# A two-layer diffusion trunk: layer 0's first feed-forward projection by seven block products instead of eight, with its results through DRAM

## The chip, the cores and the metric

The kernel runs on one core of a Trainium2 chip. The core has five engines with a queue of instructions each: TensorE (PE in the rows; its weight loads are PEld), VectorE (DVE), ScalarE (ACT), GpSimd (POOL), and SyncE (SP), which issues most DMAs. Matrix products land in PSUM (eight banks), everything else is in SBUF, inputs and outputs are in DRAM. The metric is the device time of one execution in microseconds, the median of several.

## The reference

Two layers over 512 latent and 256 context tokens of width 1024 (768 columns in the kernel, the context first). Layer 0 mixes by pooling and a recurrence, layer 1 by attention; each is followed by a SwiGLU feed-forward of hidden width 2816. Every sub-layer has a norm ahead and one behind, with shift, scale and gate worked out from the conditioning vectors `c` and `c_ctx` (the modulation). Only the latent rows are returned.

```python
def swiglu(h, w_in, w_out):
    a, b = jnp.split(h @ w_in, 2, axis=-1)
    return (jax.nn.silu(a) * b) @ w_out

for l in range(DEPTH):
    need_ctx = l < DEPTH - 1
    m_lat = (jax.nn.silu(c) @ ada_w[l] + ada_b[l])[:, None]
    m_ctx = jax.nn.silu(c_ctx) @ ada_w[l] + ada_b[l]
...
    x = x + g1 * rmsnorm(y_lat, norm_g[l, 1])
    f_lat = swiglu(rmsnorm(x, norm_g[l, 2]) * (1.0 + sc2) + sh2, ffn_w_in[l], ffn_w_out[l])
    x = x + g2 * rmsnorm(f_lat, norm_g[l, 3])
    if need_ctx:
        ctx_s = ctx_s + cg1 * rmsnorm(y_ctx, norm_g[l, 1])
        f_ctx = swiglu(rmsnorm(ctx_s, norm_g[l, 2]) * (1.0 + csc2) + csh2, ffn_w_in[l], ffn_w_out[l])
        ctx_s = ctx_s + cg2 * rmsnorm(f_ctx, norm_g[l, 3])
```

## The kernel before

Activations lie transposed: 128 features on the partitions, tokens along the row, eight tiles for the width of 1024 (index `k`). Each float32 operand of a large product is split into two float32r parts, a high one (`hi`, a rounding copy on ACT) and a low one (`lo`, the remainder, a subtraction on DVE; `split`, L570). A product of two split operands is three matmuls (`mm3`, L117: high by high, high by low, low by high), and the three lines L121 to L123 are nearly all of PE's work. Weights come from DRAM in halves of 128x1024 (`raw`, four buffers), are split into slots of 128x2048 (`w`, two of them, and `w3`, a third one in the feed-forward) and used at once.

The feed-forward of layer 0 (`ffn`, L599) goes through the 22 hidden blocks of 128 in chunks of 4, 4, 4, 4, 4 and 2 (`FCH`). A hidden block loads 128x2048 weights (the gate's half and the other one), and for the column groups 0 to 255 (context) and 256 to 767 (latent) makes two results over the eight `k` (2 x 24 matmuls for each group), a SiLU on ACT, a product on DVE and a split into tiles `gh`, `gl` in SBUF. At the end of a chunk the second projection multiplies its tiles by the weights `w_fo` and adds to the eight rows `y` (a copy on ACT for the first chunk, an addition on DVE later, L637). The first three blocks and the last two are made in groups of 256 columns, as the norms deliver or want them. The norms run beside the products as generators (`along`, `tick`): squares on ACT, sums on DVE, two small PE steps (L140, L155) with a power on POOL between them, then scaling on DVE and ACT, and the residual's addition on POOL.

Layer 1's modulation (`ada_cols`, L292) runs beside layer 0's feed-forward: 48 loads of 128x1024, and for each two DVE instructions of 1024 elements that also sum up (L297), one for the latent vector and one for the context's. After the last chunk come the last two norms of each column group, then `att_proj` (L680): queries and keys of layer 1, first for latent columns 0 to 255, then 256 to 511. The queries are written into tiles of the pool `y`.

The code names no times: a scheduler lays out each engine's queue ahead of the run, in order of the program with gaps filled. A queue is worked off in its order, and a waiting instruction holds back all behind it.

Of the kernel before, what the change touches and what calls it, by code (L numbers as in the profile page):

```python
# [15 lines left out]
D = 1024  # L16
# [16 lines left out]
FCH = (4, 4, 4, 4, 4, 2)  # L33
# [27 lines left out]
class Groups:  # L61


    def __init__(self, pool, groups):
        self.t = {}
        self.add(pool, groups)

    def add(self, pool, groups):
        for a, _ in groups:
            self.t[a // 256] = [pool.tile([128, 256], F32, tag=f"y{a // 256}_{k}", name=f"y{a // 256}_{k}") for k in range(KD)]  # L70

    def __call__(self, k, a, b):
        return self.t[a // 256][k][:, a % 256:a % 256 + b - a]
# [8 lines left out]
class Trunk:  # L82
    def __init__(self, tc, a, dbg=None, stop=None):
        self.tc, self.nc, self.a = tc, tc.nc, a
        self.dbg = dbg or {}
        self.stop = stop
        self.w3, self.nw = None, 0
# [17 lines left out]
    def wslot(self, src, n, pool=None, tag="w"):  # L105

        if pool is None:
            self.nw += 1
            pool, tag = (self.w3, "w3") if self.w3 and self.nw % 3 == 0 else (self.wp, "w")
        hi = pool.tile([128, 2048], F32R, tag=tag + "hi", name=tag + "hi")  # L110
        lo = pool.tile([128, 2048], F32R, tag=tag + "lo", name=tag + "lo")
# [5 lines left out]
    def mm3(self, out, ops, first=True, last=True):  # L117

        n = len(ops)
        for i, (wh, wl, xh, xl) in enumerate(ops):  # L120
            self.nc.tensor.matmul(out=out, lhsT=wh, rhs=xh, start=first and i == 0, stop=False)  # L121
            self.nc.tensor.matmul(out=out, lhsT=wh, rhs=xl, start=False, stop=False)  # L122
            self.nc.tensor.matmul(out=out, lhsT=wl, rhs=xh, start=False, stop=last and i == n - 1)  # L123
# [50 lines left out]
    def prenorm(self, x, h, l, which, a, b):  # L174
# [8 lines left out]
        for k in range(KD):  # L183
# [13 lines left out]
    def norm(self, x, a, b):  # L197

        ss = yield from self.sumsq(x, a, b)
        rb = self.spread(self.rms(ss, b - a, D))  # L200
        for k in range(KD):
            self.nc.vector.tensor_tensor(out=x(k, a, b), in0=x(k, a, b), in1=rb[:, :b - a], op=ALU.mult)

    def modulate(self, x, h, l, which, a, b):
# [3 lines left out]
        for k in range(KD):  # L208
            u = self.np.tile([128, 256], F32, tag="u", name="u", bufs=8)
            nc.vector.tensor_scalar(out=u[:, :n], in0=x(k, a, b), scalar1=self.scol[l][which][:, k, c:c + 1],  # L210
                                    scalar2=self.shcol(l, which, k, c), op0=ALU.mult, op1=ALU.add)
            nc.scalar.activation(out=h[0](k, a, b), in_=u[:, :n], func=AF.Copy)
            (nc.gpsimd if k % 2 else nc.vector).tensor_tensor(out=h[1](k, a, b), in0=u[:, :n],
                                                              in1=h[0](k, a, b).bitcast(F32), op=ALU.subtract)
# [47 lines left out]
    def htiles(self, ctx=True):  # L262
        return [cols(self.hcp if ctx else None, self.hlp, KD, F32R, t) for t in ("hh", "hl")]
# [28 lines left out]
    def ada_cols(self, m):  # L292

        nc = self.nc
        raw = self.load(self.a["adat"][m], 1024)
        for i in range(2):
            nc.vector.scalar_tensor_tensor(out=self.junk, in0=raw, scalar=1.0, in1=self.cb[:, i * 1024:i * 1024 + 1024],  # L297
# [4 lines left out]
    def load_cb(self, cb):  # L302
        self.cb = cb
        self.nc.sync.dma_start(out=cb, in_=self.a["cb"].partition_broadcast(128))
        self.nc.scalar.activation(out=cb, in_=cb, func=AF.Silu)

    def ada_tail(self, l, m0, m1, src):
# [3 lines left out]
        nc.vector.tensor_tensor(out=m[:, m0:m1, :], in0=src,  # L311
                                in1=self.adab[:, l * 48 + m0:l * 48 + m1].unsqueeze(2).to_broadcast([128, m1 - m0, 2]),
                                op=ALU.add)
        for o in range(m0, m1, 8):
            which, part = divmod(o // 8, 3)
            ng = self.ng[:, (l * 4 + which * 2) * 8:(l * 4 + which * 2 + 2) * 8]
            if part == 1:
                nc.vector.scalar_tensor_tensor(out=self.scol[l][which], in0=m[:, o:o + 8, :], scalar=1.0,
                                               in1=ng[:, 0:8].unsqueeze(2).to_broadcast([128, 8, 2]),
                                               op0=ALU.add, op1=ALU.mult)  # L320
            elif part == 2:
                nc.vector.tensor_tensor(out=self.gcol[l][which], in0=m[:, o:o + 8, :],
                                        in1=ng[:, 8:16].unsqueeze(2).to_broadcast([128, 8, 2]), op=ALU.mult)
# [275 lines left out]
    def ffn(self, l, y, h, order0, groups, last, done, step=0):  # L599


        nc = self.nc
        j0, slot = 0, 0
        for ci, kc in enumerate(FCH):
            g = [cols(self.gp if l == 0 else None, self.gp, kc, F32R, t) for t in ("gh", "gl")]
            w = {}

            def load(i):
                if i not in w:
                    w[i] = self.wslot(self.a["w_fi"][l, j0 + i], 2048)  # L610
                    self.ada_steps(step if ci == 1 else 0)
# [526 lines left out]
```

## Time and profile before

| | |
|---|---|
| median of 3 runs (lowest, highest) | 1637.59 us (1635.88, 1639.59) |
| the profiled execution: its time, its span | 1640.13 us, 1638.2 us |
| mean granted clock of PE | 0.989 of full |
| busy share of PE, PEld, DVE, ACT, POOL | 96%, 84%, 57%, 36%, 7% |
| matmuls | 10920 |
| DRAM traffic | 158.35 MB read, 5.24 MB written |

A matmul's busy time covers its whole passage, and the next one starts before it ends: that PE is busy says that it does not wait, and what a matmul costs is the distance from its start to that of the next. Times of the text lie on the profiled execution's axis.

### The profile page before, as it was taken

What the parts mean: (1) busy time and instruction counts of PE and PEld (TensorE: products, weight loads), DVE (VectorE), ACT (ScalarE), POOL (GpSimd) and SP (SyncE); (2) the same over time, 40 slices, a digit from 0 to 9 for tenths busy, and PEclk for the clock granted to TensorE, in tenths of its full rate; (3) what the DMA queues carried; (4) which work ended last, traced back from release to release, by engine and by line L of the source; (5) the groups of instructions that cost most, each with busy time, mean ns of one, the idle gap of its engine ahead of it and who ended that gap; (6) DMA issues with size and microseconds to landing.
All of it is one profiled execution on the core that took longest, in us unless ns stands there. A gap on an engine that the chain in (4) does not pass through costs nothing.

```text
span 1638.2 us, 26865 instructions
## 1 busy us (share of the span) xinstructions
PE 1571.3 (96%) x10920; PEld 1377.5 (84%) x10920; DVE 931.6 (57%) x1821; ACT 587.4 (36%) x1104; POOL 112.1 (7%) x147
## 2 busy tenths in 40 slices
PE   4999999999999999999999999899999999999997
PEld 1877777789998888888888898899998888888886
DVE  5466575654656566676532458778937523343345
ACT  4334343254542211212122135458845332222222
POOL 1100000001200000000000012310004000000002
PEclk9999999999999999999999999999999999999999
DMA  9242232342215444444421113230032223322311
GB/s 339 79 155 79 82 126 79 123 153 85 86 56 164 129 144 152 142 142 153 130 65 65 53 52 104 71 110 27 1 104 78 93 88 103 103 92 89 103 52 52
DMA packets 55803, 167.96 MB, mean 103 GB/s; under 512 B 7040, under 2 KB 16000, under 8 KB 55296
## 3 DMA queue, kind: packets, MB, share of 16 engines
q1 hardware_dynamic: 55536, 166.05, 31.5%
q8 instruction: 86, 1.41, 0.4%
q14 instruction: 37, 0.30, 0.1%
q10 hardware_dynamic: 144, 0.20, 0.0%
HBM read 158.35 MB, written 5.24 MB: 100 GB/s over the span
## 4 chain that ended last, share of the span: by engine, by line
PE 69%; DVE 4%; POOL 2%; issue 1%; ACT 1%; DMA 0%; POOLq 0%; DVEq 0%; ACTq 0%
PE mm L121 21%; PE mm L122 21%; PE mm L123 21%; PE pp L817 1%; DVE ss L169 1%; PE aux L155 1%; PE st L121 1%; POOL rr L146 1%; PE st L123 1%; POOL xl L231 1%; PE st L122 1%; PE aux L140 1%; DVE wlo L572 1%; DVE u L227 1%; DVE u L185 0%
## 5 line engine op out<-in xcount | busy, mean ns | idle before, releaser
L121 PE MATMUL mm<-hhl,whi 128*128 128x512 f32 (+1 forms) x944 | 325.9, 348 | 4.2 <-ACT kt L730 2.3
L122 PE MATMUL mm<-hll,whi 128*128 128x512 f32 (+1 forms) x944 | 325.6, 346 | 0.2 <-DVE hll L193 0.2
L123 PE MATMUL mm<-hhl,wlo 128*128 128x512 f32 (+1 forms) x944 | 325.2, 346 | 0.0
L571 ACT ACTIVATE whi<-raw 128x1024 fp32r<-128x1024 f32 x132 | 135.5, 1054 | 310.7 <-PE mm L122 242.2
L121 PEld LDWEIGHTS mm<-hhl,whi 128*128 128x128 f32 x944 | 179.2, 191 | 24.0 <-ACT hhl L188 2.5
L123 PEld LDWEIGHTS mm<-hhl,wlo 128*128 128x128 f32 x944 | 179.5, 191 | 20.2
L622 DVE TENSOR_TENSOR sa<-sa,mm 128x512 f32<-128x512 f32 (+1 forms) x76 | 41.0, 539 | 272.7 <-PE mm L123 272.7
L122 PEld LDWEIGHTS mm<-hll,whi 128*128 128x128 f32 x944 | 179.6, 191 | 19.6 <-DVE hll L193 0.6
L572 DVE TENSOR_TENSOR wlo<-raw,whi 128x1024 fp32r<-128x1024 f32 x132 | 160.2, 1234 | 60.3 <-ACT whi L571 57.0
L297 DVE SCALAR_TENSOR_TENSOR junk<-raw,cb 128x1024 f32<-128x1024 f32 x96 | 117.4, 1223 | 45.9 <-DMA raw<-adat 44.8
L146 POOL TENSOR_TENSOR rr<-rv,mhalf 128x2 f32<-128x2 f32 x55 | 41.9, 766 | 1473.1 <-DVE rv L143 1472.6
L637 DVE TENSOR_TENSOR y<-y,mm 128x256 f32<-128x256 f32 x200 | 76.8, 417 | 90.1 <-PE mm L123 89.5
L121 PE MATMUL mm<-hhl,w3hi 128*128 128x512 f32 (+1 forms) x336 | 117.3, 350 | 0.0
L122 PE MATMUL mm<-hll,w3hi 128*128 128x512 f32 (+1 forms) x336 | 117.3, 349 | 0.0
L123 PE MATMUL mm<-hhl,w3lo 128*128 128x512 f32 (+1 forms) x336 | 117.2, 349 | 0.0
L121 PE MATMUL mm<-ghl,whi 128*128 128x512 f32 (+1 forms) x304 | 111.1, 370 | 1.8 <-ACT ghl L571 1.8
L122 PE MATMUL mm<-gll,whi 128*128 128x512 f32 (+1 forms) x304 | 112.0, 370 | 0.0
L123 PE MATMUL mm<-ghl,wlo 128*128 128x512 f32 (+1 forms) x304 | 111.0, 367 | 0.0
L121 PE MATMUL mm<-hhc,whi 128*128 128x256 f32 x384 | 110.2, 290 | 0.1
L123 PE MATMUL mm<-hhc,wlo 128*128 128x256 f32 x384 | 109.3, 286 | 0.0
L122 PE MATMUL mm<-hlc,whi 128*128 128x256 f32 x384 | 108.7, 284 | 0.0
L621 ACT ACTIVATE sa<-mm 128x512 f32<-128x512 f32 (+1 forms) x76 | 36.4, 479 | 161.2 <-PE mm L123 161.1
(226 smaller groups left out, 3310.0 us busy)
## 6 DMA issues: line engine op xcount, KB each, us to landing
raw<-w_fi SPq DMA_DIRECT2D x88, 512.0 KB, 3.8
raw<-ada SPq DMA_DIRECT2D x48, 512.0 KB, 5.4
raw<-adat SPq DMA_DIRECT2D x48, 512.0 KB, 3.7
raw<-w_fo SPq DMA_DIRECT2D x44, 512.0 KB, 3.8
raw<-w_ab SPq DMA_DIRECT2D x20, 512.0 KB, 4.6
raw<-w_at SPq DMA_DIRECT2D x10, 512.0 KB, 4.3
xl<-x SPq DMA_DIRECT2D x16, 256.0 KB, 4.1
raw<-w_abo SPq DMA_DIRECT2D x8, 512.0 KB, 4.3
```

The lines of the kernel that those rows point to most:

```text
L121: self.nc.tensor.matmul(out=out, lhsT=wh, rhs=xh, start=first and i == 0, stop=False)
L122: self.nc.tensor.matmul(out=out, lhsT=wh, rhs=xl, start=False, stop=False)
L123: self.nc.tensor.matmul(out=out, lhsT=wl, rhs=xh, start=False, stop=last and i == n - 1)
L140: nc.tensor.matmul(out=pc[:, 2 * t:2 * t + 2], lhsT=ss[:, t * 128:(t + 1) * 128], rhs=self.ones[:, 0:2], start=True, stop=True)
L146: nc.gpsimd.tensor_tensor(out=r[:, :nt], in0=v[:, :nt], in1=self.mhalf[:, :nt], op=ALU.pow)
L155: nc.tensor.matmul(out=pb[:, t * 128:(t + 1) * 128], lhsT=r[:, t:t + 1].to_broadcast([128, 128]), rhs=self.ident, start=True, stop=True)
L297: nc.vector.scalar_tensor_tensor(out=self.junk, in0=raw, scalar=1.0, in1=self.cb[:, i * 1024:i * 1024 + 1024], op0=ALU.mult, op1=ALU.mult, ...
L571: self.nc.scalar.activation(out=hi, in_=src, func=AF.Copy)
L572: (eng or self.nc.vector).tensor_tensor(out=lo, in0=src, in1=hi.bitcast(F32), op=ALU.subtract)
L621: nc.scalar.activation(out=s[:, :n], in_=p[0][:, :n], func=AF.Silu)
L622: nc.vector.tensor_tensor(out=s[:, :n], in0=s[:, :n], in1=p[1][:, :n], op=ALU.mult)
L637: nc.vector.tensor_tensor(out=yt, in0=yt, in1=p, op=ALU.add)
```

## The change

The first projection of layer 0's hidden blocks 3 to 20 is made by Winograd's form of Strassen's product (`wino_w`, `wino_x`, `wino_hidden`). Weights, tokens and features are halved: the weight block becomes four 128x512 pieces, the activations four blocks of 512 features by 384 tokens. Instead of eight products of such blocks there are seven, of 12 matmuls of 384 columns each; three of the seven weight pieces are sums of others (four additions on DVE), four of the activation operands are sums, made once (`t1` to `t4`, `wino_x`), and the results are put together by seven DVE instructions and two copies on ACT. All seven weight pieces are split. Two additions are saved by letting a second product accumulate onto a bank that was read before (`first=False`).

Blocks 0 to 2 are made as before, block 21 in two groups of 384 columns. All hidden results are written to DRAM (`gd`, one tile of 128x2x768 for each block) and read back by POOL's DMA queue for the second projection, which comes after all first projections, in chunks of 7, 8, 3 and 4 blocks. The residual `x` goes out to DRAM (`x1`) after the first norm and is read back at the end. The norm ahead of the feed-forward writes its unsplit result into `y` (`raw`), from which `wino_x` reads.

Other parts: at the start `x` is loaded by 4 DMAs of long rows instead of 16, its squares are summed over all 768 columns at once, and the first half of the value weights is loaded ahead of the last modulation step. Layer 1's modulation leaves out the context's part where nothing uses it (64 DVE instructions instead of 96): 24 columns run beside the seven-product blocks, 24 beside the second projection. `h`, `y` and the queries lie in tiles of all 768 columns (`Full`).

```diff
-FCH = (4, 4, 4, 4, 4, 2)
+FCH = ((7, 8, 3, 4), (4, 4, 4, 4, 4, 2))
...
+    def wino_w(self, src):
...
+        put("a11", a11)
+        s1 = total("s1", a21, a22)
+        r2 = total("r2", s1, a11)
+        put("r2", r2)
+        put("s1", s1)
+        put("a12", a12)
+        put("r3", total("r34", a11, a21))
+        put("r4", total("r34", a12, r2))
+        put("a22", a22)
...
+    def wino_x(self, y, pool):
...
+        for k in range(H):
+            b11, b12, b21, b22 = y(k, 0, n), y(k, n, NT), y(k + H, 0, n), y(k + H, n, NT)
...
+            nc.vector.tensor_tensor(out=r[1], in0=b11, in1=b12, op=ALU.subtract)
+            nc.vector.scalar_tensor_tensor(out=r[2], in0=r[1], scalar=-1.0, in1=b22, op0=ALU.mult, op1=ALU.subtract)
+            nc.vector.tensor_tensor(out=r[3], in0=b22, in1=b12, op=ALU.subtract)
+            for i in (2, 1, 3):
+                self.split(t[i][0][k], t[i][1][k], r[i])
...
+            nc.vector.tensor_tensor(out=r4, in0=b21, in1=r[2], op=ALU.add)
+            self.split(t[4][0][k], t[4][1][k], r4)
...
+    def wino_hidden(self, w, h, t, put):
...
+        prod(pa, "a11", blk(0, 0))
+        nc.scalar.activation(out=q1, in_=pa[:, :n], func=AF.Copy)
+        prod(pb, "r2", t[2])
+        add(u, q1, pb[:, :n])
+        prod(pc, "s1", t[1])
+        nc.scalar.activation(out=q5, in_=pc[:, :n], func=AF.Copy)
+        prod(pa, "a12", blk(H, 0), False)
+        nc.scalar.activation(out=s, in_=pa[:, :n], func=AF.Silu)
+        prod(pb, "r3", t[3], False)
+        add(q1, q1, pb[:, :n])
+        add(q5, q5, q1)
+        prod(pc, "r4", blk(H, n), False)
+        add(u, u, pc[:, :n])
+        nc.scalar.activation(out=u, in_=u, func=AF.Silu)
+        prod(pd, "a22", t[4])
+        nc.vector.scalar_tensor_tensor(out=u, in0=u, scalar=-1.0, in1=q5, op0=ALU.mult, op1=ALU.mult)
+        put(n, NT, u)
+        add(q1, pd[:, :n], q1, ALU.subtract)
+        add(s, s, q1, ALU.mult)
+        put(0, n, s)
...
+                self.split(t[:, 0, :b - a], t[:, 1, :b - a], src)
+                nc.sync.dma_start(out=gd[j][:, :, a:b], in_=t[:, :, :b - a].bitcast(F32))
...
+        for j in range(3, KH - 1):
+            self.wino_hidden(self.wino_w(self.a["w_fi"][0, j]), h, t, put(j))
...
+                nc.gpsimd.dma_start(out=t, in_=gd[j].bitcast(F32R))
...
+            g = [two([gload(j, j) for j in range(7)])]
+            wl = self.wslot(self.a["w_fi"][0, KH - 1], 2048)
+            for a, b in SG:
+                self.hidden(wl, h, a, b, put(KH - 1))
...
+                for a, b in GL + GS[:1]:
+                    for n in range(KD):
+                        self.outs(0, 3, g[3], y, n, wo[n // 4], a, b)
+                        self.tick(4 * 0.32)
+                    self.along((a, 0), done(x, h1, a, b))
...
-        self.q = Groups(yp, GL)
+        self.q = Full(yp, KD, F32, "y")
```

PE's queue where hidden block 3 is reached, before: the end of its context group and the start of its latent group (`hhc`, `hhl` are the high parts of the activations, `hlc`, `hll` the low ones).

```order
L121 MATMUL mm<-hhc_3704,w3hi 128x256
L122 MATMUL mm<-hlc_3720,w3hi 128x256
L123 MATMUL mm<-hhc_3704,w3lo 128x256
L121 MATMUL mm<-hhl_3705,w3hi 128x512
L122 MATMUL mm<-hll_3721,w3hi 128x512
L123 MATMUL mm<-hhl_3705,w3lo 128x512
```

The same place after the change (`hh`, `hl` the activations themselves, `t1` and `t2` the sums of `wino_x`):

```order
L187 MATMUL mm<-hh_3515,w3lo 128x384
L185 MATMUL mm<-hh_3516,w3hi 128x384
L186 MATMUL mm<-hl_3524,w3hi 128x384
L187 MATMUL mm<-hh_3516,w3lo 128x384
L185 MATMUL mm<-hh_3517,w3hi 128x384
L185 MATMUL mm<-t2h_5002,w3hi 128x384
L186 MATMUL mm<-t2l_5006,w3hi 128x384
L185 MATMUL mm<-t1h_4994,w3hi 128x384
L186 MATMUL mm<-t1l_4998,w3hi 128x384
L187 MATMUL mm<-t1h_4994,w3lo 128x384
L185 MATMUL mm<-t1h_4995,w3hi 128x384
L187 MATMUL mm<-t2h_5002,w3lo 128x384
```

Four matmuls of the fourth product have moved ahead of the second one, and the second and third products stand interleaved, `k` by `k`.

DVE's queue beside one hidden block of the dense part, before: the product with the SiLU, the low parts of results and weights, and the modulation's sums.

```order
L622 TENSOR_TENSOR sa<-sa,mm 128x256
L297 SCALAR_TENSOR_TENSOR junk,mods_101<-raw,cb 128x1024
L572 TENSOR_TENSOR glc_5724<-sa,ghc_5716 128x256
L297 SCALAR_TENSOR_TENSOR junk,mods_101<-raw,cb 128x1024 x2
L622 TENSOR_TENSOR sa<-sa,mm 128x512
L572 TENSOR_TENSOR wlo<-raw,whi 128x1024 x2
L572 TENSOR_TENSOR gll_5728<-sa,ghl_5720 128x512
L297 SCALAR_TENSOR_TENSOR junk,mods_101<-raw,cb 128x1024
L622 TENSOR_TENSOR sa<-sa,mm 128x256
L297 SCALAR_TENSOR_TENSOR junk,mods_101<-raw,cb 128x1024
```

Beside hidden block 4 after the change, from the evacuation of its second product (`u`) to that of its fifth (`q`):

```order
L699 TENSOR_TENSOR u_5447<-q_5445,mm 128x384
L642 TENSOR_TENSOR w3lo<-raw,w3hi 128x512
L146 TENSOR_TENSOR s_5568<-raw 128x512
L642 TENSOR_TENSOR wlo<-raw,whi 128x512
L146 TENSOR_TENSOR r_5570<-s_5568,raw 128x512
L642 TENSOR_TENSOR wlo<-s_5568,whi 128x512
L146 TENSOR_TENSOR r_5578<-raw 128x512
L642 TENSOR_TENSOR w3lo<-r_5570,w3hi 128x512
L366 SCALAR_TENSOR_TENSOR raw,mods_101<-raw,cb_5090 128x1024
L699 TENSOR_TENSOR q_5445<-q_5445,mm 128x384
L642 TENSOR_TENSOR wlo<-r_5578,whi 128x512
L699 TENSOR_TENSOR q_5446<-q_5446,q_5445 128x384
```

Between the evacuations of the second and the fifth product stand seven instructions that make ready weight pieces of block 5 (`s`, `r` are sums of weights) and a modulation sum.

POOL's queue at the end of the mixer's norms, before: the residual's additions and the norm's power.

```order
L231 TENSOR_TENSOR xl_3655<-xl_3655,u 128x256
L231 TENSOR_TENSOR xl_3656<-xl_3656,u 128x256
L146 TENSOR_TENSOR rr<-rv,mhalf 128x2 x2
L231 TENSOR_TENSOR xl_3649<-xl_3649,u 128x256
L231 TENSOR_TENSOR xl_3650<-xl_3650,u 128x256
L231 TENSOR_TENSOR xl_3651<-xl_3651,u 128x256
```

POOL's queue after the change, at the end of the first projections:

```order
L786 DMA g_7888<-gd_4427 128x1536
L786 DMA g_7890<-gd_4428 128x1536
L806 DMA hh_8023<-gd_4429 128x768
L806 DMA hl_8031<-gd_4429 128x768
L806 DMA hh_8024<-gd_4430 128x768
L806 DMA hl_8032<-gd_4430 128x768
L806 DMA hh_8025<-gd_4431 128x768
```

POOL now issues 30 DMAs in a row, the seven `g` of the first chunk, then 16 into the tiles of `h`, then seven more; the norms' powers and additions of the last part stand behind them.

## Rows read from the trace of the kernel before

**Rows 1.** The page: busy time by engine; PE's busy tenths in 40 slices.

```profile
PE 1571.3 (96%) x10920; PEld 1377.5 (84%) x10920; DVE 931.6 (57%) x1821; ACT 587.4 (36%) x1104; POOL 112.1 (7%) x147
...
PE   4999999999999999999999999899999999999997
```

**Rows 2.** Windows: stretch, length, busy of PE, PEld, DVE, ACT, POOL, clock, DMA.

```profile
347.70:464.00 116.30, 112.68 (x881) 108.07 (x880) 68.08 (x136) 59.11 (x129) 23.10 (x30) 0.99 0.32 105
464.00:938.10 474.10, 474.10 (x2788) 421.80 (x2787) 264.02 (x448) 106.05 (x167) 0.00 (x0) 1.00 0.39 120
955.70:1089.00 133.30, 121.80 (x884) 114.39 (x882) 98.29 (x264) 62.29 (x142) 39.80 (x51) 0.97 0.28 84
1089.00:1199.00 110.00, 109.80 (x815) 108.44 (x816) 95.58 (x235) 86.48 (x181) 1.37 (x2) 0.97 0.08 25
```

**Rows 3.** Timeline of PE: start, duration, line, tiles, shape; dense runs of three widths.

```profile
537.90 0.28 PE L121 MATMUL mm<-hhc,w3hi 128*128 128x256 f32 x1
...
543.17 0.28 PE L123 MATMUL mm<-hhc,w3lo 128*128 128x256 f32 x1
543.29 0.39 PE L121 MATMUL mm<-hhl,w3hi 128*128 128x512 f32 x1
...
553.99 0.39 PE L123 MATMUL mm<-hhl,w3lo 128*128 128x512 f32 x1
...
1119.84 0.34 PE L121 MATMUL st<-kh,qh 128*128 128x384 f32 x1
...
1120.71 0.34 PE L123 MATMUL st<-kh,ql 128*128 128x384 f32 x1
```

**Rows 4.** Groups on DVE, whole run: count, busy us, mean ns, idle before it.

```profile
L572 DVE TENSOR_TENSOR wlo<-raw,whi 128x1024 fp32r<-128x1024 f32 x132 | 160.2, 1234 | 60.3 <-ACT whi L571 57.0
...
L572 DVE TENSOR_TENSOR pl<-pp,ph 128x384 fp32r<-128x384 f32 x64 | 33.8, 549 | 3.3 <-ACT ph L571 2.9
...
L622 DVE TENSOR_TENSOR sa<-sa,mm 128x512 f32<-128x512 f32 x34 | 23.4, 687 | 209.0 <-PE mm L123 209.0
...
L297 DVE DVE_READ_ACCUMULATOR junk<-raw,cb 128x1 f32 x96 | 7.9, 82 | 0.0
```

**Rows 5.** Timeline of DVE, back-to-back instructions: start, duration, line, tiles.

```profile
706.67 0.41 DVE L637 TENSOR_TENSOR y<-y,mm 128x256 f32<-128x256 f32 x1
707.00 0.69 DVE L572 TENSOR_TENSOR gll<-sa,ghl 128x512 fp32r<-128x512 f32 x1
707.61 1.22 DVE L572 TENSOR_TENSOR w3lo<-raw,w3hi 128x1024 fp32r<-128x1024 f32 x1
...
712.30 1.22 DVE L297 SCALAR_TENSOR_TENSOR junk<-raw,cb 128x1024 f32<-128x1024 f32 x1
...
713.57 1.22 DVE L297 SCALAR_TENSOR_TENSOR junk<-raw,cb 128x1024 f32<-128x1024 f32 x1
```

**Rows 6.** Groups on ACT, whole run: count, busy us, mean ns, idle before it.

```profile
L571 ACT ACTIVATE ph<-pp 128x384 fp32r<-128x384 f32 x64 | 28.5, 490 | 1.5 <-PE pp L817 1.1
...
L571 ACT ACTIVATE ghl<-sa 128x512 fp32r<-128x512 f32 x34 | 20.9, 614 | 0.0
```

**Rows 7.** Timeline of DVE: norms of latent columns 0 to 255 after the feed-forward.

```profile
956.05 0.42 DVE L637 TENSOR_TENSOR y<-y,mm 128x256 f32<-128x256 f32 x1
...
964.01 1.88 DVE L227 SCALAR_TENSOR_TENSOR u<-y,gcol,aux 128x256 f32<-128x256 f32 x4 [0.80 <-PE aux L155]
...
983.57 0.48 DVE L185 SCALAR_TENSOR_TENSOR u<-xl,scol,aux 128x256 f32<-128x256 f32 x1
...
991.93 0.48 DVE L193 SCALAR_TENSOR_TENSOR hll<-u,mods,hhl 128x256 fp32r<-128x256 f32 x1
```

**Rows 8.** DMA issues, whole run: tiles, queue, count, KB each, median us to landing.

```profile
raw<-w_fi SPq DMA_DIRECT2D x88, 512.0 KB, 3.8
...
xcs<-xc SPq DMA_DIRECT2D x1, 1024.0 KB, 3.9
...
xc<-xcs SPq DMA_DIRECT2D x1, 1024.0 KB, 4.9
```

More of the change, by code (lines that the diff above doesn't have):

```diff
@@ L105, in wslot @@
     def wslot(self, src, n, pool=None, tag="w"):
[L107 to L111, printed above, removed]
+        hi, lo = self.wtile(pool, tag)
         for a in range(0, n, 1024):
@@ L115, in wslot, with wtile, piece @@
         return hi, lo
-    def mm3(self, out, ops, first=True, last=True):
-        n = len(ops)
+    def wtile(self, pool=None, tag="w"):
+        if pool is None:
+            self.nw += 1
+            pool, tag = (self.w3, "w3") if self.w3 and self.nw % 3 == 0 else (self.wp, "w")
+        return [pool.tile([128, 2048], F32R, tag=tag + t, name=tag + t) for t in ("hi", "lo")]
+    def piece(self):
+        if not self.left:
+            w = self.wtile()
+            self.left = [[t[:, o:o + 512] for t in w] for o in range(0, 2048, 512)]
+        return self.left.pop(0)
@@ L260, in finish, with htiles @@
                 pass
[L262 to L263 removed]
+    def htiles(self):
+        return [Full(self.hlp, KD, F32R, t) for t in ("hh", "hl")]
     def shcol(self, l, which, k, c):
@@ L597, in outproj, with hidden @@
                 self.along(a, done(a, b))
-    def ffn(self, l, y, h, order0, groups, last, done, step=0):
+    def hidden(self, w, h, a, b, put):
         nc = self.nc
-        j0, slot = 0, 0
-        for ci, kc in enumerate(FCH):
-            g = [cols(self.gp if l == 0 else None, self.gp, kc, F32R, t) for t in ("gh", "gl")]
+        n = b - a
+        p = [self.ps(), self.ps()]
+        for q in range(2):
+            self.mm3(p[q][:, :n], self.ops(w, q * 1024, h, a, b))
+        s = self.sm.tile([128, 512], F32, tag="sa", name="sa")
+        nc.scalar.activation(out=s[:, :n], in_=p[0][:, :n], func=AF.Silu)
+        nc.vector.tensor_tensor(out=s[:, :n], in0=s[:, :n], in1=p[1][:, :n], op=ALU.mult)
+        put(a, b, s[:, :n])
+        self.tick(n / 50)
@@ new lines, in outs, with fo @@
+    def outs(self, l, ci, g, y, n, slot, a, b):
+        nc, kc = self.nc, FCH[l][ci]
+        pt = self.ps()
+        self.mm3(pt[:, :b - a], self.ops(slot, n % PER[kc] * kc * 128, g, a, b, 0, kc))
+        if ci == 0:
+            nc.scalar.activation(out=y(n, a, b), in_=pt[:, :b - a], func=AF.Copy)
+        else:
+            nc.vector.tensor_tensor(out=y(n, a, b), in0=y(n, a, b), in1=pt[:, :b - a], op=ALU.add)
+    def fo(self, l, ci, n):
+        per = PER[FCH[l][ci]]
+        i = sum(KD // PER[k] for k in FCH[l][:ci]) + n // per
+        return self.wslot(self.a[f"w_fo{l}"][i], per * FCH[l][ci] * 128)
@@ L606, in ffn @@
+    def ffn(self, l, y, h, order0, groups, last, done):
+        j0 = 0
+        for ci, kc in enumerate(FCH[l]):
+            g = [cols(None, self.gp, kc, F32R, t) for t in ("gh", "gl")]
             w = {}
```

331 lines of the change are left out of this document (206 added, 125 removed).

## Prediction

> **What bounds the kernel now.** First the page's busy line: PE is busy for 96% of the span, DVE 57%, ACT 36% [rows 1]. Such shares are averages, so next the windows by stage. Over most of layer 0's feed-forward PE is busy for all of the 474.10 us, while DVE works 264.02 of them and the DMA engines 39% at 120 GB/s; the clock is granted in full (1.00) [rows 2]. PE never waits there. So nothing that is taken from DVE, ACT or DMAs in this stage shortens it, and every matmul that goes, or gets shorter, does, as long as the other engines deliver. PE does wait at two borders of the stage: ahead of it, from 347.7 to 464, 3.6 us; behind it, from 955.7 to 1089, 11.5 us [rows 2]. Those are the places where a new wait could be added to an old one.
>
> What a matmul costs is not its busy time but the distance from start to start, which the dense timeline gives: 44 steps from 537.90 to 543.17 are 0.120 us for 256 columns, 47 steps from 543.29 to 553.99 are 0.228 us for 512, and 5 steps from 1119.84 to 1120.71 are 0.174 us for 384 [rows 3]. The last lies halfway between the others, so the cost is a fixed 0.012 us and 0.42 ns a column.
>
> **The saving.** A hidden block of the old form is 48 matmuls of 512 columns and 48 of 256: 48 x 0.228 + 48 x 0.120 = 16.7 us. A block of seven products is 7 x 12 = 84 matmuls of 384: 84 x 0.174 = 14.6 us. Of the 18 blocks concerned, 17 (3 to 19) had the old form and block 20 was one of the two at the end made in groups of 256: 144 x 0.120 = 17.3 us. Before, 17 x 16.7 + 17.3 = 300.8 us with unrounded steps; after, 18 x 14.6 = 263.1: minus 37.7. Block 21 goes from 144 x 0.120 to 96 x 0.174 = 16.7: minus 0.5. The last output chunk is now 4 blocks and not 2 in groups of 256; 48 matmuls of 512 become 96 of 256: plus 0.6. **Net: minus 37.6 us.** This assumes that PE goes on without waiting; the rest of the sum is what could end that.
>
> **The operands t1 to t4.** Before, block 3 needed only what the norms had written. Now the second product needs `wino_x`, that is 32 DVE instructions of 384 columns behind the last of the norm, and its latent tail. Back to back a DVE instruction of 256 takes 0.33 us and one of 512 takes 0.61 [rows 5], so 384 about 0.47: 15 us. Ahead of and between them stand the norm's last instructions (some 12 of 256 at 0.42 to 0.48 [rows 5, 7], about 5.5 us), the eight instructions for the four results of the running blocks (8 x 0.33 = 2.6), and the first weight pieces of block 3 (about six of 512, 3.7): 27 us in all. PE has work for 4 results of 48 matmuls of 256 columns meanwhile, 4 x 5.75 = 23 us. The order shows that the scheduler itself fills this place: products two and three are interleaved, and matmuls of the fourth are put ahead. Plus 4 us, between 0 (all of it starts earlier) and 8 (by full durations, 32 x 0.549 [rows 4]).
>
> **The dense part with seven products.** Per block DVE has 7 low parts and 4 sums of weights (512 columns, 11 instructions), 7 evacuations and 2 low parts of results (384, 9 instructions), and 1.62 modulation sums of 1024 while those last, some 15 blocks (24 columns, 9.0 to 14.6 in the pacing). Back to back: 11 x 0.61 + 9 x 0.47 + 1.62 x 1.27 [rows 5] = 13.0 us, 89% of PE's 14.6. By full durations, 11 x 0.687 + 9 x 0.549 + 1.62 x (1.22 + 0.082) [rows 4, 5] = 14.6 us, 100%. The timeline decides for the first: the evacuation of 256 columns starts 0.33 us ahead of its follower though it lasts 0.41 [rows 5].
> The Trainium skill ("VectorE: DVE Perf Modes", section "The DRAIN you can't avoid") says that the next instruction does not start until the pipe has emptied; it also says that one which is not held starts earlier. Read strictly it would put DVE at PE's own length, and the reserve would be nil; [rows 5] sides with the exception.
> The nearest stage with such a load is the attention, 1089 to 1199: DVE busy 95.58 of 110.00 us, 87%, and PE busy 109.80 [rows 2]. So a DVE near 90% can leave PE unhurt, where the queue's order fits. In the new order seven weight and modulation instructions stand between two evacuations, about 4.9 us back to back (6 x 0.61 + 1.27), while the banks are to be used again two or three products of 2.1 us later: tight, not impossible. ACT has 7 copies of 512, 2 copies for results and 4 evacuations of 384: 7 x 0.614 + 6 x 0.490 [rows 6] = 7.2 us, half of a block. DMA moves 1 MB of weights, 0.79 MB of results and 0.81 MB of modulation weights per 14.6 us, 2.6 MB or 178 GB/s; the share of 39% at 120 GB/s [rows 2] makes that 58%. Plus 2 us over the stage, between 0 and 15.
>
> **The results through DRAM.** The writes hang on nobody but the two buffers `gs`. Reading back matters once: the first output chunk needs seven tiles of 768 KB on POOL's queue. A read-back from DRAM of 1024 KB took 4.9 us and a write 3.9 [rows 8]: 3.7 us for 768 KB, 26 for seven. They may start as block 20 frees the `t` tiles, some 10 us before its end, and PE has block 21 (16.7 us) besides: 27 us. If one landing per 3.8 us for 512 KB [rows 8] is the pace, they take 40 us: plus 13. The sixteen loads behind them have the first chunk's own 7 x 24 x (0.228 + 0.120) = 58 us, and are covered. Plus 1 us, between 0 and 13.
> The Trainium skill ("DMA: Bandwidth & Descriptors", section "Anatomy of one DMA — SWDGE (gpsimd) path") fits 2.0 us and the bytes at 436 GB/s for one DMA on POOL's path; an estimate from it is 3.8 us each and 26.6 us for seven in a row, and the sum would stay as it is. No POOL DMA lies in this trace.
>
> **The end of the feed-forward.** From the last output addition (956.05) to the last low part (991.93 + 0.48) the norms of latent columns 0 to 255 take 36.4 us [rows 7]. Before, PE worked on other column groups beside it and still lost 11.5 us in this stage [rows 2]. Now the last chunk has 4 blocks: each group of 256 gives 8 x 12 x 0.120 = 11.5 us of cover, and two groups follow: 23 us, so 13 us stay open, against the 11.5 lost already. Further, the queries are written into the rows `y`, whose context columns must have gone through the last norm first; with four banks in turn the fifth query waits for that. Against it, keys and values of the context come earlier into reach. Plus 5 us, between minus 5 and plus 15.
>
> **The rest.** The norm's unsplit result costs one more instruction per `k` and group (ACT's 0.49 [rows 6], 8 of them in a chain that ends in the 3.6 us of waiting before 464): plus 1, 0 to 3. At the start, longer rows and fewer DMAs speak for a gain, 1 MB of value weights ahead of the last modulation step against it (3.9 us or so for 1024 KB [rows 8]): 0, minus 3 to plus 3. The 32 modulation sums left out, 32 x 1.27 [rows 5] = 41 us of DVE, are no time of the path, since PE did not wait; they are what makes room for the added DVE work.
>
> **Sum.** Minus 37.6 + 4 + 2 + 1 + 5 + 1 + 0 = minus 24.6. From the profiled execution's 1640.1 that gives 1615.5; the median of the runs lies 2.5 lower, so **1613 us**.
>
> **Rivals.**
> (a) All covered: the new waits vanish beside other work, as the attention's DVE at 87% with PE at 109.80 of 110.00 [rows 2] suggests, and the cover at both borders holds: minus 37.6, that is 1600 (1596 to 1605). Against it: 27 us to do in 23, and the shorter cover at the end.
> (b) DVE becomes the bound of the seven-product stage, the slower side. A low part waits for its high part on ACT: 57.0 us over 132 of them, 0.43 us each [rows 4]. If each of nine low parts per block does so, 13.0 becomes 16.9 and 14.6 becomes 18.5 us per block over 15 blocks, 34 to 58 us more than PE's 14.6, and the sum without the stage's 2 is minus 26.6: 1645 to 1669. It ends slower when DVE needs over 14.6 + 26.6/15 = 16.4 us per block. For it: evacuations queue behind weight work in the new order. Against it: today's wait ends are idle time of a DVE that had nothing else, and the order mixes independent instructions between.
> (c) The read-back is late. At the 26 us above nothing happens; the time is lost when seven tiles take over 27 + 24 us, 108 GB/s, as on a queue that delivers one at a time with other loads beside it. At half the pace of [rows 8]'s first row, 80 us, it is plus 53: 1666. At its full pace, 1626.
>
> **Chances.** The forecast's mechanism, small stalls at the borders (1604 to 1630): 0.58. (a) 0.18. (b) 0.15, of which 0.09 slower, 0.02 same, 0.04 faster because the wait is only partial. (c) 0.09: 0.03 slower, 0.01 same, 0.05 faster. About 0.2% (1634.3 to 1640.9) is what a measurement of this kernel can tell from no change; 0.01 of the forecast's own lies in it and 0.01 beyond, by an end at its worst. Faster 0.56 + 0.18 + 0.04 + 0.05 = 0.83, same 0.01 + 0.02 + 0.01 = 0.04, slower 0.01 + 0.09 + 0.03 = 0.13. Range: the forecast's 0.58 and (a), with the mild ends of (b) and (c), about 0.85: 1597 to 1638; the forecast's own range is 1604 to 1630.
>
> **What the profile after would show.** Matmuls of 384 columns 0.174 us apart and a period of about 14.6 us per block with PE busy throughout: the saving. A period of 15 or more, with PE waiting for DVE's `u` or `q`, or for `w...lo`: rival (b). A gap of PE of about 4 us at the first product with `t2`; one ahead of the first output, ended by a POOL DMA: rival (c). Between the last output and the first dense queries 10 to 20 us without PE, ended by the norm or by `y`. Wrong above all would be the sum if the seven products' operands arrive in an order that leaves PE idle in each block: 1 us in each is 18.

## The result and the profile after

The changed kernel takes 1648.03 us (median of 4 runs, 1646.77 to 1650.64) against 1638.59 before: ratio 1.0062, 95% interval 1.0043 to 1.0081, slower by 9.4 us. The forecast was 1613, in a range of 1597 to 1638. The profiled execution has a span of 1648.6 us, before 1638.2.

The page first, PE's line, its tenths and the granted clock; these answer to [rows 1]:

```profile
PE 1545.3 (94%) x10656; PEld 1385.3 (84%) x10656; DVE 1004.0 (61%) x1923; ACT 647.0 (39%) x1228; POOL 122.6 (7%) x163
...
PE   5999998999999999999599994999999999999997
...
PEclk9999999999999999999799996999999899999998
```

PE has 264 matmuls less and is busy for 26 us less, yet the span is 10.4 us longer, and the tenths have two holes that [rows 1] doesn't have: a 5 in slice 20 and a 4 in slice 25, with the clock down beside them. The windows show these places and the seven-product stage ahead of them (stretch, length, busy of PE, PEld, DVE, ACT, POOL, clock, DMA share and GB/s):

```profile
515.26:752.06 236.80, 236.80 (x1345) 236.80 (x1345) 201.74 (x363) 107.97 (x207) 1.50 (x3) 1.00 0.53 174
775.00:789.70 14.70, 14.70 (x86) 12.81 (x84) 1.11 (x2) 1.77 (x4) 5.44 (x11) 1.00 1.11 376
789.70:809.30 19.60, 0.38 (x2) 0.00 (x0) 7.31 (x12) 3.47 (x4) 0.00 (x0) 0.60 0.91 306
809.30:830.00 20.70, 20.67 (x110) 18.33 (x111) 16.45 (x25) 5.53 (x9) 0.00 (x0) 0.88 0.73 217
...
964.20:1097.50 133.30, 107.45 (x749) 101.67 (x747) 95.63 (x255) 59.34 (x132) 42.87 (x50) 0.88 0.31 93
```

The first window is 16 hidden blocks: 14.80 us each, PE busy all the time, DVE 85% busy, DMAs at 174 GB/s. PE waits for nothing there. The next ones are the border to the second projection: DMAs at 376 GB/s, then 19.6 us in which PE does nothing, then 20.7 us at a mean clock of 0.88, which is another 2.5 (20.7 x 0.12, an estimate). The last window is the 133.30 us ahead of the first attention product, as long as the one of before that ends at 1089 [rows 2]: PE is idle for 133.30 - 107.45 = 25.9 us of it, before 133.30 - 121.80 = 11.5, and the clock is 0.88, before 0.97.

The chain of waits through the first hole (start, length, what):

```profile
777.75 0.51 SPq L373
778.32 0.68 SPq L80
779.04 5.59 SPq L80
784.68 18.56 DMA raw<-adat
803.26 1.24 DVE junk L366 x2
804.52 3.68 DMA raw<-w_fo
808.22 1.06 ACT whi L641
809.33 0.58 PE mm L185
```

It is not the read-back for the first chunk: no row of `g` stands in the chain. PE waits for the output weights of rows 2 and 3 (`whi`). They come in 3.7 us once they are issued, but SP issues them at 804.52 only. Ahead of them in SP's queue stand the conditioning vector's load (L373), two loads of the residual (L80) and two of the modulation (`adat`); the weights need a `raw` buffer that becomes free when the modulation's sums have run (L366), and the load that these sums waited for took 18.56 us. The DMA issues of 748 to 810 suggest why (tiles, queue, count, KB each, median us to landing):

```profile
hh<-gd POOLq DMA_DIRECT2D x8, 384.0 KB, 10.3
hl<-gd POOLq DMA_DIRECT2D x8, 384.0 KB, 11.4
...
x<-x SPq DMA_DIRECT2D x2, 1024.0 KB, 21.8
...
cb<-cb SPq DMA_DIRECT2D x1, 1024.0 KB, 11.6
```

From 771.90 to 786 POOL issues the second chunk's 16 read-backs, 6.3 MB that no matmul reads before 856. With the loads of the residual and of the conditioning vector (3 MB) they fill the DMA engines. That this is the reason is so far an argument; `e3_readback_later` and `e5_mod_and_readback` try it.

At the second hole three waits of PE stand out (with the idle time ahead of a row and what ended it):

```profile
998.48 0.58 PE L187 MATMUL mm<-hh,wlo 128*128 128x256 f32 x1 [3.10 <-DVE wlo L642]
...
1014.02 0.98 PE L204 MATMUL aux<-ones,ss 128*128 128x2 f32 x4 [6.94 <-DVE ss L233]
...
1026.02 0.58 PE L185 MATMUL mm<-hh,whi 128*128 128x256 f32 x1 [8.69 <-ACT y L912]
```

The second is the sum of squares of the context's norm, the third the evacuation of the first queries. ACT's own queue at that time:

```profile
1024.49 0.72 ACT L232 ACTIVATE sq<-x 128x256 f32<-128x256 f32 x2 [0.72 <-DVE ss L233]
1025.21 0.38 ACT L910 ACTIVATE sq<-mm 128x256 f32<-128x256 f32 x1
1025.49 0.47 ACT L912 ACTIVATE y<-mm,consts 128x256 f32<-128x256 f32 x1
```

The queries' evacuations (L910, L912) stand right behind the context norm's last squares (L232).

At the first block of seven products PE waits once, for ACT's copy of the first product (`q`):

```profile
494.01 0.44 PE L185 MATMUL mm<-hh,w3hi 128*128 128x384 f32 x1 [1.39 <-ACT q L705]
```

The sum of the 10.4 us between the spans: seven products, 18 x 14.80 against the 300.8 worked out for before, minus 34.4; the wait at the first of them with what follows it, 1.7; the first hole with its clock, 19.25 + 2.5 = 21.7; the second border, 14.4 more idle and, from the matmuls' distances in the two windows, about 1.5 for the clock (an estimate); from the first attention product to the end 551.1 against 549.2, plus 1.9. That makes 6.8. Most of the other 3.6 lies ahead of block 3, which begins at 490.37 here and at 487.21 before. The same code reaches it between 484.38 and 490.37 in the profiled executions of this kernel and of the ten experiments, so this part is no more than spread.

### The profile page after: what moved, and what is told of

It reads as the page before. It is cut to its first block, busy times and chain, and to the rows that moved or that the text cites. A ratio compares the mean times of both kernels' runs of the same rounds, so it can differ in the third digit from the quotient of the medians.

```text
span 1648.6 us, 26592 instructions
## 1 busy us (share of the span) xinstructions
PE 1545.3 (94%) x10656; PEld 1385.3 (84%) x10656; DVE 1004.0 (61%) x1923; ACT 647.0 (39%) x1228; POOL 122.6 (7%) x163
## 4 chain that ended last, share of the span: by engine, by line
PE 62%; DVE 6%; POOL 2%; ACT 2%; issue 1%; DMA 1%; SPq 0%; POOLq 0%; DVEq 0%; ACTq 0%
PE mm L185 20%; PE mm L186 19%; PE mm L187 19%; DVE ss L233 1%; DMA raw<-adat 1%; PE pp L1022 1%; POOL x L298 1%; PE aux L204 1%; PE aux L219 1%; PE st L185 1%; PE st L187 1%; PE st L186 1%; DVE u L294 0%; DVE wlo L642 0%; POOL rr L210 0%
## 5 line engine op out<-in xcount | busy, mean ns | idle before, releaser
L185 PE MATMUL mm<-hh,whi 128*128 128x256 f32 (+2 forms) x1292 | 431.1, 335 | 9.9 <-ACT y L912 8.7
L187 PE MATMUL mm<-hh,wlo 128*128 128x256 f32 (+2 forms) x1292 | 427.1, 331 | 5.0 <-DVE wlo L642 3.3
L186 PE MATMUL mm<-hl,whi 128*128 128x256 f32 (+2 forms) x1292 | 426.9, 331 | 0.0
L185 PEld LDWEIGHTS mm<-hh,whi 128*128 128x128 f32 x1292 | 247.5, 192 | 39.4 <-ACT y L912 9.0
L187 PEld LDWEIGHTS mm<-hh,wlo 128*128 128x128 f32 x1292 | 247.7, 192 | 23.0 <-DVE wlo L642 3.7
L186 PEld LDWEIGHTS mm<-hl,whi 128*128 128x128 f32 x1292 | 247.8, 192 | 16.5 <-DVE hl L642 0.2
L641 ACT ACTIVATE whi<-raw 128x1024 fp32r<-128x1024 f32 (+2 forms) x145 | 134.1, 945 | 227.9 <-PE mm L186 118.9
L642 DVE TENSOR_TENSOR wlo<-raw,whi 128x1024 fp32r<-128x1024 f32 (+2 forms) x145 | 156.6, 1096 | 70.8 <-ACT whi L641 69.3
L678 DVE TENSOR_TENSOR sa<-sa,mm 128x256 f32<-128x256 f32 (+2 forms) x38 | 20.7, 546 | 165.3 <-PE mm L187 165.2
L185 PE MATMUL mm<-hh,w3hi 128*128 128x256 f32 (+2 forms) x284 | 94.1, 332 | 2.8 <-ACT w3hi L641 1.4
L186 PE MATMUL mm<-hl,w3hi 128*128 128x256 f32 (+2 forms) x284 | 93.7, 331 | 0.0
L366 DVE SCALAR_TENSOR_TENSOR raw<-raw,cb 128x1024 f32<-128x1024 f32 x48 | 58.4, 1220 | 5.5 <-DMA raw<-adat 4.9
```

Source lines behind the costliest of these rows:

```text
L366: nc.vector.scalar_tensor_tensor(out=junk, in0=raw, scalar=1.0, in1=self.cb[:, i * 1024:i * 1024 + 1024], op0=ALU.mult, op1=ALU.mult, accu ...
L641: self.nc.scalar.activation(out=hi, in_=src, func=AF.Copy)
L642: (eng or self.nc.vector).tensor_tensor(out=lo, in0=src, in1=hi.bitcast(F32), op=ALU.subtract)
L678: nc.vector.tensor_tensor(out=s[:, :n], in0=s[:, :n], in1=p[1][:, :n], op=ALU.mult)
```

## The experiments

The runs of one edited kernel spread by up to 10 us, those of the kernel before by 16 in one series, and up to 6 us arise ahead of block 3, where nothing was edited. So each edit is read from its own stage first and from the median second. Four matmuls of the changed kernel part the stages: the first of block 3, the first of the output chunks, the first of the second chunk and the first of attention.

```profile
490.37 0.34 PE L185 MATMUL mm<-hh,w3hi 128*128 128x384 f32 x1
...
775.08 0.28 PE L185 MATMUL mm<-g,w3hi 128*128 128x256 f32 x1
...
856.05 0.28 PE L185 MATMUL mm<-hh,whi 128*128 128x256 f32 x1
...
1097.53 0.69 PE L185 MATMUL st<-kh,qh 128*128 128x384 f32 x1 [1.71 <-DVE rv L207]
```

The hidden blocks from 3 on thus take 284.71 us, the first chunk (the first border) 80.97, and the rest up to attention (the second border) 241.48.

**Was the saving there?** `e1_eight` makes the same blocks by eight products, all else left (the sums t1 to t4 are made and not used):

```diff
-            self.wino_hidden(self.wino_w(self.a["w_fi"][0, j]), h, t, put(j))
+            w8 = self.wslot(self.a["w_fi"][0, j], 2048)
+            for a, b in SG:
+                self.hidden(w8, h, a, b, put(j))
```

> The changed kernel, but hidden blocks 3 to 20 are made by eight products (two groups of 384 columns, weights split as before); the sums t1 to t4 are still made and not used; all else, DRAM route included, stays. Theory A (the saving was there in full and was lost elsewhere): a block takes 96 x 0.174 = 16.7 us instead of 14.6, 18 blocks 37.6 us; the two stalls of PE near 790 and 980 to 1026 stay. 1648 + 37 = 1683 to 1687 us. Rival B (the seven-product stage itself gave back part of its saving): less than 30 us slower, under 1678.

Measured: 1682.52 us, ratio to the kernel before (here and below) 1.026 (1.0233 to 1.0287), 34.5 more than the changed kernel, half a microsecond under theory A's range. The hole of 19.25 us stands there unchanged, from 820.9 to 840.2, and the second border's 133.3 us have PE busy for 106.90:

```profile
840.19 0.58 PE L185 MATMUL mm<-g,whi 128*128 128x256 f32 x1 [19.25 <-ACT whi L641]
```

```profile
994.10:1127.40 133.30, 106.90 (x754) 101.27 (x752) 92.98 (x253) 57.74 (x130) 42.17 (x50) 0.88 0.28 85
```

So the losses have nothing to do with the seven products, as theory A says. The stage itself puts the saving lower than the median does: the hidden blocks take 316.17 us in `e1_eight` and 284.71 in the changed kernel, 31.5 less, just over rival B's bound of 30; the other 3 us of the median's 34.5 lie outside the edited stage. The 31.5 are net of the 1.7 at the first product. The rest of the miss to 37.6 is mostly in the step from matmul to matmul. In `e1_eight` 7 steps of 384 columns take 1.21 us, 0.173 each; with seven products one block follows the other after 14.80 us, 84 steps of 0.176 on average (here the start of the fifth product, in blocks 8 and 9 of the changed kernel):

```profile
699.69 0.33 PE L187 MATMUL mm<-hh,w3lo 128*128 128x384 f32 x1
...
700.90 0.33 PE L185 MATMUL mm<-hh,w3hi 128*128 128x384 f32 x1
```

```profile
559.66 0.34 PE L185 MATMUL mm<-t3h,whi 128*128 128x384 f32 x1
...
574.46 0.34 PE L185 MATMUL mm<-t3h,w3hi 128*128 128x384 f32 x1
```

**The first hole: order or crowding?** `e2_mod_later` starts the modulation's second half behind the weights of rows 2 and 3:

```diff
-                self.along("ada", ada1(0, 24, 5.5))
...
+                        if ci == 0 and n == 2:
+                            self.along("ada", ada1(0, 24, 5.0))
```

> The changed kernel, but layer 1's second half of the modulation starts at the third row of the first output chunk, not ahead of the chunk. Theory A (the 19.65 us stall at 790 is one of queue order: the output weights of rows 2 and 3 stand on SyncE behind modulation loads, which wait for buffers that the modulation's sums free late): SyncE can now issue these weights ahead of block 21's stores, the stall goes with the slower clock behind it: 1648 - 22 = 1624 to 1629. Rival B (whatever is loaded there is late, since the read-back fills the DMA engines): the next pair of weights is late instead and PE waits over 10 us there: over 1636.

`e3_readback_later` keeps that order and holds POOL's 16 read-backs until row 1 is evacuated:

```diff
+                            nc.vector.tensor_copy(out=gb[p](k, 0, 1), in_=y(1, 0, 1))
                             nc.gpsimd.dma_start(out=gb[p](k, 0, NT), in_=gd[7 + k][:, p, :].bitcast(F32R))
...
+                        if ci == 0 and n == 1:
+                            gbload()
```

> The changed kernel, but the 16 read-backs for the second output chunk (6.3 MB) wait until row 1 of the first chunk is evacuated (16 added DVE copies of one column make them wait); the order of modulation and weights on SyncE stays. Theory A1 (the modulation load that held the weights took 18.6 us because the DMA engines were full with these read-backs): it lands in 4 to 6 us, the weights are issued near 790 and the stall shrinks to 4 to 8 us: 1632 to 1637. Rival B1 (order alone; the sums wait for the conditioning vector's load and SiLU anyway): the stall stays over 12 us, 1640 to 1648.

Measured: 1633.74 us (0.9958, 0.9943 to 0.9974) and 1637.14 us (0.9984, 0.9968 to 1.0001), 14 and 11 less than the changed kernel. The first chunk takes 68.20 and 70.57 us, 12.8 and 10.4 less. PE's wait in the one and in the other:

```profile
805.23 0.56 PE L185 MATMUL mm<-g,whi 128*128 128x256 f32 x1 [5.08 <-ACT whi L641]
```

```profile
797.07 0.58 PE L185 MATMUL mm<-g,whi 128*128 128x256 f32 x1 [9.13 <-ACT whi L641]
```

Neither theory is enough. With the order mended the next pair of weights is late by 5.08 us, for the same reason (its chain has a modulation load of 20.51 us):

```profile
778.33 20.51 DMA raw<-adat
798.87 1.25 DVE junk L366 x2
800.13 3.97 DMA raw<-w_fo
```

With the read-back held back 9.13 us remain, one more than the most that theory A1 allowed. That is not queue order alone. The edit lets the read-backs start at 784.80 in place of 771.90; the residual's loads then land after a median of 8.9 us (21.8 without the edit), but the modulation load still takes 10.32 us, not 4 to 6, and the weights behind it 6.55:

```profile
777.78 10.32 DMA raw<-adat
...
789.38 6.55 DMA raw<-w_fo
```

So how the 19.25 us divide between order and crowding stays open. `e5_mod_and_readback` has both edits.

> The changed kernel with both edits of the runs e2_mod_later and e3_readback_later. If the two causes (weights behind modulation loads in SyncE's queue; those loads slowed by the read-back) are all of the stall near 790, none of the 9.5 and 5.5 us that each alone left remains: the border costs under 2 us, 1625 to 1630. If the DMA engines lack time whatever the order, 5 us or more stay: over 1632.

Measured: 1626.23 us, 0.9906 (0.9889 to 0.9924). The first chunk takes 59.36 us, 21.6 less: the hole and its slower clock are gone whole. At the place of the hole, 783 to 803, PE is busy throughout, although the DMAs now move 392 GB/s there:

```profile
783.00:803.00 20.00, 20.00 (x116) 17.48 (x116) 10.38 (x30) 6.24 (x9) 7.56 (x15) 1.00 1.12 392
```

So the two causes together are all of it, and full DMA engines alone cost nothing here, since what PE needs next isn't behind them.

**The second border: the queries.** `e4_queries` gives their squares buffers of their own and writes the queries into the present rows `y` in place of a new allocation:

```diff
-                sq = self.np.tile([128, 256], F32, tag="sq", name="sq", bufs=self.sb)
+                sq = self.np.tile([128, 256], F32, tag="sqq", name="sqq", bufs=2)
...
-        self.q = Full(yp, KD, F32, "y")
+        self.q = y
```

> The changed kernel, but layer 1's queries have buffers of their own for their squares (two, instead of sharing three with the norms), and are written into the same rows y instead of a new allocation of them, so that a query waits for its own columns alone. Theory C (the waits near 1007 and 1017 come from query evacuations on ScalarE that stand behind the context norm's squares, through the shared buffers and the rows): ScalarE's queue has them ahead, PE's gaps of 7.2 and 9.1 us shrink to the norm steps' own, and the stage's clock recovers: 8 to 14 us faster, 1634 to 1640. Rival D (the norm chain of the second latent group and the context bounds the stage, whatever the queries do): the gaps move to the next query group, under 4 us gained, over 1644.

`e6_squares_only` has the first of the two edits alone.

> The changed kernel with only the first half of e4_queries: the queries' squares have two buffers of their own; the queries still go into a new allocation of the rows y. Theory C1 (the evacuations stood behind the context norm's squares through the shared buffers): the gain of e4_queries is here already, 1639 to 1644, and the 9.1 us gap is gone. Theory C2 (the rows y, as the prediction had it: a query waits for the context's last norm to have read them): little is gained, 1645 to 1650, and the gap stays.

Measured: 1641.95 us (0.9998, 0.9976 to 1.0021) and 1639.75 us (0.9995, 0.9979 to 1.0011). The windows of the last 133.30 us ahead of attention, in `e4_queries` and `e6_squares_only`, answer to 107.45 us of PE in the changed kernel:

```profile
953.10:1086.40 133.30, 111.42 (x794) 105.44 (x792) 96.38 (x255) 60.10 (x134) 41.43 (x51) 0.92 0.30 91
```

```profile
953.20:1086.50 133.30, 112.94 (x788) 106.92 (x787) 96.73 (x259) 59.57 (x133) 42.74 (x51) 0.90 0.30 92
```

`e4_queries` lies between the ranges of theory C and rival D, `e6_squares_only` in that of theory C1. The squares alone bring 5.5 us of PE's time back, both edits 4.0; from the second chunk to attention the two kernels take 4.7 and 5.4 us less than the changed one. So the squares are nearly all of the gain and the rows at most 0.7 us: theory C1. The dependency that the prediction had named does exist, but it is small; in `e6_squares_only` a query's copy waits for the context's last norm (L294), and PE waits for such copies 1.7 us in all where it was 8.7:

```profile
1011.57 0.47 ACT L912 ACTIVATE y<-mm,consts 128x256 f32<-128x256 f32 x1 [5.37 <-DVE u L294]
```

In `e4_queries` the wait moves in part to the norm's own step in PE's queue, which is rival D's share:

```profile
1021.96 0.99 PE L204 MATMUL aux<-ones,ss 128*128 128x2 f32 x4 [11.33 <-DVE ss L233]
```

**The second border: the cover.** `e7_more_cover` makes the last output chunk 6 blocks and not 4:

```diff
-FCH = ((7, 8, 3, 4), (4, 4, 4, 4, 4, 2))
+FCH = ((7, 8, 1, 2, 2, 2), (4, 4, 4, 4, 4, 2))
...
-                        self.outs(0, 3, g[3], y, n, wo[n // 4], a, b)
+                        self.mm3(pt[:, :b - a], [o for i in range(3) for o in self.ops(wo[i], n * 256, g[3 + i], a, b, 0, 2)])
```

> The changed kernel, but the output chunks are 7, 8, 1 and 6 blocks instead of 7, 8, 3 and 4 (the last one from three weight slots of two blocks each): a column group of the last chunk takes 8 x 18 x 0.120 = 17.3 us instead of 11.5, so 34.6 us of products follow the first latent group's last output instead of 23. Theory E (the lost cover costs up to 11.5 us of the 15.9 that this stage lost): 8 to 12 us faster, 1636 to 1641. Rival F (all three weight slots are busy until the last output, so the query weights are late, or the chain of three norms bounds the stage whatever lies beside it): under 4 us, over 1644.

Measured: 1638.73 us (0.9992, 0.9976 to 1.0008). PE is busy for 113.87 of the last 133.30 us, 6.4 more than in the changed kernel. The median's 9 us contain the start's spread; from the second chunk to attention it is 5.5 us less. The stage thus says about 6, between theory E and rival F:

```profile
953.90:1087.20 133.30, 113.87 (x797) 107.96 (x795) 92.21 (x248) 57.95 (x129) 38.79 (x47) 0.89 0.31 93
```

**All four edits** (`e8_all`).

> All four edits together: modulation later, read-back later, queries with their own squares and in place, last output chunk of 6 blocks. If the losses are separate they add: 20 at the first border, 14 at the second: 1612 to 1620, below both kernels; the saving of the seven products then shows nearly whole. If the edits at the second border share one chain of norms, only the larger counts there: 1618 to 1624.

Measured: 1614.64 us (1612.4 to 1617.2), ratio 0.9836 (0.9815 to 0.9856), 24 us under the kernel before. The first chunk takes 59.36 us. The window of the first border has no wait, and the last 133.30 us have PE busy for 116.91:

```profile
766.00:806.00 40.00, 40.00 (x234) 36.02 (x234) 14.28 (x36) 9.34 (x15) 8.56 (x16) 1.00 0.87 305
```

```profile
929.90:1063.20 133.30, 116.91 (x840) 111.41 (x838) 94.02 (x248) 58.48 (x132) 39.71 (x50) 0.92 0.30 91
```

At the second border the edits of `e4_queries` and `e7_more_cover` nearly add: in PE's busy time 4.0 and 6.4 alone, 9.5 together; in the length from the second chunk to attention 5.4 and 5.5 alone, 10.6 together. The largest wait left is 9.93 us for the context's sum of squares:

```profile
998.39 0.99 PE L204 MATMUL aux<-ones,ss 128*128 128x2 f32 x4 [9.93 <-DVE ss L233]
```

Behind it in PE's queue stand query products, which then start without a wait of their own; whether they could have run earlier no run shows.

**DVE's reserve.** `e9_dve_plus3` and `e10_dve_plus9` put three and nine more DVE instructions of 384 columns among the evacuations of each seven-product block, one or three at each of three places:

```diff
+        def fill(x):
+            for _ in range(3):
+                jw = tp.tile([128, n], F32, tag="jw", name="jw", bufs=1)
+                add(jw, x, x, ALU.max)
...
         add(u, q1, pb[:, :n])
+        fill(u)
```

> The changed kernel with three more DVE instructions of 384 columns in each seven-product block (a maximum of a tile with itself into a tile that nobody reads), among the evacuations. DVE is busy 237.42 of 275.00 us there, 12.8 us of each block's 14.8. Theory G (an instruction costs its distance from the next one, 0.47 us for 384): 12.8 + 1.4 = 14.2 us, still under 14.8; the block stays at 14.8 to 14.9 and the time within 3 us of the changed kernel. Rival H (it costs its full duration of 0.55 us, and the queue's order already uses up the reserve): 14.6 + 1.6 = 16.3 us per block in 15 blocks, 20 to 25 us slower.

> The same with nine more such instructions in each block. Theory G: 12.8 + 9 x 0.47 = 17.0 us in the 15 blocks with modulation sums, 15.0 in the other three, DVE is then the bound: a block takes about 17, 15 x 2.2 + 3 x 0.2 = 34 us slower, 1677 to 1688. Rival H: 14.6 + 4.9 = 19.5 us per block, 60 to 70 us slower, over 1705.

Measured: 1649.59 us (1.0053, 1.0032 to 1.0074) and 1688.24 us (1.0285, 1.0261 to 1.031). The windows of 16 blocks, three more and nine more:

```profile
514.19:750.99 236.80, 236.80 (x1346) 236.80 (x1346) 224.64 (x414) 110.96 (x208) 1.51 (x3) 1.00 0.54 175
```

```profile
511.96:789.82 277.86, 251.59 (x1345) 244.05 (x1345) 269.43 (x516) 113.94 (x210) 1.50 (x3) 0.95 0.46 149
```

With three more DVE is busy for 95% of the stage and the block is still 14.80 us: theory G, and H is out. With nine more DVE is the bound (97% of a stage in which PE waits), a block takes 277.86 / 16 = 17.4 us and the whole 40 us more. That is 6 over G's 34 and far under H's 60; the excess is not broken down.

## Why the prediction was wrong, point by point

- **The saving** (minus 37.6): right in kind, 34.4 by the period of 14.80 us per block, and 31.5 net in `e1_eight`, where a block of eight products takes 16.64. The term's step of 0.174 for 384 columns was 0.176. The reason is not known: three more DVE instructions per block leave the period at 14.80, and the same shape with eight products has 0.173. It isn't the summed operands alone: the mean step is 0.1765 with `t1` to `t4` and 0.1757 with the activations themselves.
- **The operands t1 to t4** (plus 4): 1.7. The scheduler's interleaving covered them; the wait was for ACT's evacuation of the first product.
- **The dense part** (plus 2, and rival (b)): nothing. The price by start-to-start distances was right; DVE still had at least the room for three instructions of 384. Between the two evacuations stand eight instructions, not the seven counted (7 x 0.61 + 1.27 = 5.5 us, not 4.9), and PE did not wait for them either. By the rule of the Trainium skill ("VectorE: DVE Perf Modes", section "The DRAIN you can't avoid"), read strictly, DVE would have had no reserve, and `e9_dve_plus3` would have cost 20 us or more (an estimate); it cost 1.6, and the trace sides with the rule's exception. Rival (b) would have needed more than three further instructions per block; with nine it is there.
- **The results through DRAM** (plus 1): this is the step that failed most, by 20.7 us. The first seven tiles came in time, so rival (c), as written, didn't happen either. What failed is the sentence that the sixteen loads behind them "are covered". The term asked when somebody needs them, and not whom they delay. They took the DMA engines from a modulation load (18.56 us; the median of all 48 is 4.4); this load held a `raw` buffer, the output weights behind it on SP had to wait for that buffer, and PE for the weights: 21.7 us with the clock. The queues shown with the change had POOL's 30 DMAs in a row, and the prediction looked only at POOL's queue for them. The other half of the cause is SP's queue, where the modulation loads stand ahead of the weights; no term of the prediction had it. Each edit alone leaves 5 to 9 us, both together nothing. The Trainium skill's fit ("DMA: Bandwidth & Descriptors", section "Anatomy of one DMA — SWDGE (gpsimd) path") gives 2.9 us for one of the 384 KB read-backs, an estimate; with so many in flight the trace has medians of 10.3 and 11.4.
- **The end of the feed-forward** (plus 5, minus 5 to 15): about 16, past the upper end: the second step that failed, by 11 us. The prediction set the 13 us of missing cover off against the 11.5 already lost; the measured idle time is 25.9, near the sum of both. `e7_more_cover` gives 6 back by more cover. The second half of the reason was wrong: not the rows `y` held the queries, but buffers for squares that they share with the norms, and with them ACT's queue (`e6_squares_only`).
- **The start and the prenorm** (0 and 1): within the spread of executions; no run tries these terms by themselves.

With the two borders mended the time comes near the forecast's: 1614.64 measured in `e8_all`, 1613 forecast. That it is so near is luck in part: the saving was 3 smaller, t1 to t4 and the dense part 4 cheaper, and `e8_all` is not the kernel that was forecast, since its last chunk is longer.

## What to carry to other kernels

A load that is prefetched far ahead of its need is not free because it is early: ask which loads share the DMA engines with it, which buffers those hold, and what stands behind them in their queue. Where work of second rank (a modulation, a residual) shares a queue and a ring of buffers with PE's next weights, put the weights first in both; here either edit alone left 5 to 9 us of a 19 us hole. And scratch buffers that two chains share put one chain's queue order on the other: two kilobytes per partition for the queries' squares were worth about 5 us.

## What the runs showed of the hardware

- DVE busy for 224.64 of 236.80 us beside a PE that never waited: 95% is not yet a bound where the order fits.
- With the DMA engines at 376 GB/s (the changed kernel, 775 to 789.7) and 382 (`e2_mod_later`, 778 to 799), 512 KB modulation loads took 18.56 and 20.51 us, where the median of all 48 is 4.4; two 1 MB loads took a median of 21.8. At 392 GB/s in `e5_mod_and_readback` (783 to 803) four modulation loads had a median of 8.5, so the rate alone does not tell the delay.
- After 19.6 us nearly without work PE's granted clock is 0.88 in the mean over the next 20.7 us, which costs 2.5 us on top of the hole; without the hole it is 1.00 there.
- Matmuls of 384 columns: 0.173 us apart in two-group blocks, 0.176 in the mean in seven-product blocks. In `e1_eight` (530 to 760) all 1325 steps are 0.173 or 0.174; in the changed kernel's 16 blocks they range from 0.170 to 0.185, with a mean of 0.1765 on `t1` to `t4` and 0.1757 on the activations. The cause is open.
